# Combining a token's two expert rows: one plain gather added by PE with the identity, one adding gather onto LN1 output loaded at the 25th expert

## The chip, the cores and the metric

The kernel runs on 1 core of one Trainium2 chip. The metric is device time in microseconds (us), lower is better. Three runs of the kernel before gave 1243.73, 1244.65 and 1237.64 us: median 1243.73.

## The reference, cut to what matters

One decoder layer over 1024 tokens (and 16 meta tokens) of width 1024: a token mixer (stick-breaking attention beside a gated delta rule), a LayerNorm (LN1), then a mixture of experts and a second LayerNorm (LN2). Each token goes to the best 2 of 8 experts inside the best 1 of 4 groups, so to 2 of 32 experts:

```python
h = layer_norm(DEEPNORM_ALPHA * h + mix, ln1_g[i], ln1_b[i])
ffn = hierarchical_moe(h.reshape(b * l, D_MODEL), ...)   # sum over a token's two experts of
                                                         # gate * (silu(x @ w1) * (x @ w3)) @ w2
h = layer_norm(DEEPNORM_ALPHA * h + ffn, ln2_g[i], ln2_b[i])
```

All is float32. The part that the change touches is the sum of a token's LN1 output `h`, its two expert rows, and the LN2 behind it.

## The kernel before

Up to some 810 us the kernel does the mixer, LN1 (its output goes to the DRAM buffer `h1d`) and the routing. Then `phase4` runs over the 32 experts, `e` = 0 to 31, in an order written out by hand (`manual_schedule`), and `finish` does the combination and LN2 for 8 tiles of 128 tokens, `t` = 0 to 7.

**Experts.** An expert has up to 128 token slots. Its tokens are gathered from `h1d` by an indirect DMA on POOL (L1499, three experts ahead), transposed on PE, multiplied with w1 and w3 (`up`: the float32 pieces 6 and 7 straight from the loaded weights on L1527, the others as a high and a low part, L1531 to L1533), and with w2 (`down`, L1559 to L1561). ACT and DVE split each loaded weight piece into its two parts (L1462, L1463). The result, times the gate, is stored to the DRAM buffer `ysd` (`keep`, L1572, on POOL) for experts 0 to 29; the rows of the last two experts stay in SBUF (`ys`) and are brought to their tokens by PE with 0/1 matrices `oh` in `finish`.

**Weights.** `load_raw` (L1437) issues the 96 weight loads of 1 MiB on SP's queue: for each expert two halves of w1 and w3, then w2. They go round a ring of 17 buffers: 4 of a pool left over from the mixer (`wo4h`, `wo4l`, `wo6h`, `wo6l`), RA = 5 (`rawa`), RB = 6 (`rawb`), RC = 2 (`rawc`). A load into a buffer waits until the load of 17 before it has been split. L1630 keeps the ring full at the end of each expert.

**Combination.** `rb.close()` (L1641) frees `rawb` and `rawc` behind the loop, and the pool `fin` takes their place. Into it SP loads the 8 tiles `yts[t]` from `h1d` (L1648) and the LN2 gain and bias `g2`, `b2` (L1650). POOL then issues, for t below GE = 5, two indirect gathers with an add for each tile (`combine`, L1574 to L1578): row k = 0 and row k = 1 of each token from `ysd`, both added by the DMA onto `yts[t]`:

```python
for k in range(2):
    nc.gpsimd.indirect_dma_start(out=yts[t], ..., in_=src, in_offset=...fi[:, t, k:k + 1]..., compute_op=ALU.add)
```

Both write the same tile, so the second waits until the first has landed. `fi` (L1603) holds the row numbers; a row out of bounds is skipped. The call of `overflow` (L1664) is a branch taken only when an expert has more than 128 tokens; inside it `yts` is written too.

**finish.** For each tile: `total` (PE brings the last two experts' rows into PSUM, `pf`; DVE adds `yts[t]`, L1773), `square` (ACT), `rstd` (DVE L100 and POOL L101), `shift` (which first issues the gathers of tile t + GE through `more`, then L1785), `scale` (ACT L119), `gain` (DVE L1791), `store` (DVE L1794, then the DMA out, L1795). The order is by `t + TO[i]` with the offsets `TO = (0, 0.75, 1.25, 2.5, 3.25, 4, 4.75)` (L37, L1798): `total(4)` stands ahead of `gain(0)` and `rstd(3)`, and so on. POOL's queue in `finish` is: rstd(0), rstd(1), gathers of tile GE, rstd(2), gathers of tile GE + 1, rstd(3), and on.

Of the kernel before, what the change touches and what calls it, by code (L numbers as in the profile page):

```python
# [8 lines left out]
F32 = mybir.dt.float32  # L9
# [3 lines left out]
ALU = mybir.AluOpType  # L13
# [33 lines left out]
YB = 2  # L47
GE = 5
SPK = ()
# [9 lines left out]
MB, BB, WB, TB = 2, 2, 2, 3  # L59
RA, RB, RC = 5, 6, 2  # L60
RT = 2
GB = 3 * HA * DH
# [18 lines left out]
class Trunk:  # L81
# [738 lines left out]
    def phase2(self):  # L820
# [241 lines left out]
        self.h1d = self.dram.tile([SEQ, D], F32, name="h1d")  # L1062
        self.ysd = self.dram.tile([(NE - 2) * P, D], F32, name="ysd")
        self.ovd = self.dram.tile([16 * P, D], F32, name="ovd")
# [372 lines left out]
    def load_raw(self, n=1, eng=None):  # L1437
        order = [(0, 0), (0, 1)] + [w for e in range(1, NE) for w in ((e, 0), (e, 1), (e - 1, 2))] + [(NE - 1, 2)]
        for _ in range(n):
            i = len(self.raws)  # L1440
            if i == 3 * NE:
                return
            j = i % (RA + RB + 4 + RC) - 4
            if j < 0:
                raw = self.wp.tile([P, 4, 512], F32, name=f"wo{8 + j // 2 * 2}{'hl'[j % 2]}")
            else:
                k = 0 if j < RA else 1 if j < RA + RB else 2
                raw = self.rawp[k].tile([P, 4, 512], F32, name="raw", bufs=(RA, RB, RC)[k])
            e, c = order[len(self.raws)]
            (eng or self.nc.sync).dma_start(raw, self.a["w13"][e][:, c * 4:c * 4 + 4] if c < 2 else self.a["w2"][e])  # L1450
            self.raws[e, c] = raw
# [23 lines left out]
    def phase4(self):  # L1475
# [9 lines left out]
        for i in range(XN):  # L1485
            x = xp.tile([P, D], F32, name=f"xg{i}")
            nc.scalar.activation(x, self.ones[:, 0:1].to_broadcast([P, D]), AF.Copy, scale=0.0)
            XB.append(x)

        def loads(w13, w2):  # L1490
# [82 lines left out]

        def combine(src, fi, n, t):  # L1574
            for k in range(2):
                nc.gpsimd.indirect_dma_start(out=yts[t], out_offset=None, in_=src,  # L1576
                                             in_offset=bass.IndirectOffsetOnAxis(ap=fi[:, t, k:k + 1], axis=0),
                                             bounds_check=n * P - 1, oob_is_err=False, compute_op=ALU.add)  # L1578

# [5 lines left out]

        pcs = {0: self.pcs0}

        def gat_(e):
# [13 lines left out]
        nc.vector.tensor_scalar(fo, self.pose, float(P), 4096.0, op0=ALU.is_ge, op1=ALU.mult)  # L1602
        nc.vector.tensor_tensor(fi, fv, fo, op=ALU.add)  # L1603
        xt = xsplit(xpose(XB[0]))
        gat_(XN)
        self.load_raw(2 + RC - RX)
        for e in range(NE):
# [12 lines left out]
            else:  # L1620
# [8 lines left out]
                evac2(yo, self.gsl[:, e - 1:e], ys[0])  # L1629
            self.load_raw(max(0, 5 + 3 * e + RA + RB + 4 + RC - len(self.raws)))  # L1630
            if e == NE - 6:
# [7 lines left out]
            if e == NE - 2:  # L1639
                oh = [xp.tile([P, NT, P], F32R, name=f"xg{i}") for i in (2, 0)]  # L1640
        self.rb.close()  # L1641
        fin = ExitStack()
        fp = fin.enter_context(self.pool("fin", "left"))
        g2, b2 = [fp.tile([P, D], F32, name=n) for n in ("g2", "b2")]
        ys.append([fp.tile([P, D], F32R, name=f"y{x}") for x in "hl"])
        yts = [fp.tile([P, D], F32, name=f"yt{t}") for t in range(NT)]
        for t in range(NT):
            nc.sync.dma_start(yts[t], self.h1d[t * P:(t + 1) * P, :])  # L1648
        for v, n in ((g2, "ln2_g"), (b2, "ln2_b")):
            nc.sync.dma_start(v, self.bcast(a[n], D))  # L1650
        for t in range(GE):
            combine(self.ysd, fi, NE - 2, t)
        evac2(down(act, pcs.pop(NE - 1)), self.gsl[:, NE - 1:], ys[1])
# [9 lines left out]

        self.overflow(item, ps, fp.tile([P, D], F32, name="xo"), combine)  # L1664
        pss.close()
        sq = mp.tile([P, KT, P], F32R, name="xh", bufs=1).rearrange("p a b -> p (a b)")
        self.finish(fp, g2, b2, yts, oh, ys, sq, lambda t: t < NT and combine(self.ysd, fi, NE - 2, t))
        fin.close()
        es.close()
        self.wos.close()  # L1670

    def overflow(self, item, ps, xo, combine):
        nc, tc, a = self.nc, self.tc, self.a
        nv = nc.values_load(self.nov[0:1, 0:1], min_val=0, max_val=16)
        pose, oh, val, slots, ob, nx = self.pose, self.oh, self.val, self.slots, self.ob, self.nx
        with tc.If(nv > 0), self.pool("ovf", "left") as vp:
# [63 lines left out]
            with tc.For_i(0, nv) as i:  # L1740
# [7 lines left out]
                     xi, xg, xo, yi)  # L1748
            for t in range(NT):
                combine(self.ovd, fi, 16, t)  # L1750

    def finish(self, fp, g2, b2, yts, oh, ys, sq, more):
        nc, tc = self.nc, self.tc
        st = [fp.tile([P, 4], F32, name=f"st{t}") for t in range(NT)]
        rs = [fp.tile([P, 2], F32, name=f"rs{t}") for t in range(NT)]
        with self.psum("psf") as ps, tc.manual_schedule():
            pfs = {}

            def part(t, j0):
                if j0 == 0:  # L1760
                    pfs[t] = ps.tile([P, D], F32, name="pf", bufs=4)
                for c in range(2):
                    for j in (j0, j0 + 1):
                        nc.tensor.matmul(pfs[t][:, c * 512:(c + 1) * 512], oh[j // 2][:, t],
                                         ys[j // 2][j % 2][:, c * 512:(c + 1) * 512], start=(j == 0), stop=(j == 3))

            part(0, 0)
            part(1, 0)
            def total(t):
                if t > 1:  # L1770
                    part(t, 0)
                part(t, 2)
                nc.vector.scalar_tensor_tensor(yts[t], pfs.pop(t), 1.0, yts[t], op0=ALU.mult, op1=ALU.add,  # L1773
                                               accum_out=st[t][:, 0:1])
# [84 lines left out]
```

## Time and profile before

| | |
|---|---|
| median of three runs | 1243.73 us (1237.64 to 1244.65) |
| the profiled execution's own time | 1243.68 us |
| its span in the trace | 1241.9 us |
| busy in the span: PE, DVE, ACT, POOL | 1079.4, 863.0, 631.0, 292.4 us |
| q1 (SP's DMA queue), share of the 16 DMA engines | 55.5% |
| q0 (POOL's DMA queue), share of the 16 DMA engines | 8.9% |

The times of rows are from the span's start; 1.8 us of the execution's own time lie outside the span. Busy shares are means over stages that differ: the expert loop runs from some 820 to 1130 us, the combination behind it to the end. `<-` behind an idle time names what ended it.

### The profile page before, as it was taken

The numbers are of one execution on the slowest core, as the hardware profiler recorded it, in microseconds if no ns is written. First come the engines' busy times: TensorE is split into PE (matmuls) and PEld (weight loads), VectorE is DVE, ScalarE is ACT, GpSimd is POOL, SyncE is SP. The second block draws the span as 40 slices with busy tenths as digits, with TensorE's granted clock in tenths as the row PEclk, the third lists the DMA queues.
The fourth block names the chain that finished last, engine by engine and source line by source line (L and its number), as shares of the span: only waits on it lengthen the run. The fifth ranks groups of instructions, "written<-read, shape, count | busy, mean of one in ns | idle before, by whom it ended". The sixth has DMA issues, their size and how long they took to land. (4 is left out here: it accounts for less than half of the span.)

```text
span 1241.9 us, 19751 instructions
## 1 busy us (share of the span) xinstructions
PE 1079.4 (87%) x7029; PEld 930.2 (75%) x7029; DVE 863.0 (69%) x1671; ACT 631.0 (51%) x1310; POOL 292.4 (24%) x389
## 2 busy tenths in 40 slices
PE   6999999999899988989899998579999999996030
PEld 5999999999799867777677777457777777774020
DVE  7931358988232378989577777869999999994045
ACT  3443437754233345655365542347777777772042
POOL 3523003402000033344243220021111111203331
PEclk8999999999899978999899997879999999999565
DMA  8411124485985676874675717669999999934645
GB/s 282 175 54 44 60 91 121 136 247 174 251 233 163 229 247 203 231 240 127 190 184 138 276 69 295 227 234 385 401 396 401 400 405 412 376 147 133 105 83 152
DMA packets 112439, 270.74 MB, mean 218 GB/s; under 512 B 31140, under 2 KB 60588, under 8 KB 99538
## 3 DMA queue, kind: packets, MB, share of 16 engines
q1 hardware_dynamic: 100816, 236.43, 55.5%
q0 software_dynamic: 11232, 31.95, 8.9%
q8 instruction: 57, 0.93, 0.3%
q10 hardware_dynamic: 290, 1.07, 0.2%
q14 instruction: 44, 0.36, 0.1%
HBM read 213.83 MB, written 64.53 MB: 224 GB/s over the span
## 5 line engine op out<-in xcount | busy, mean ns | idle before, releaser
L185 PE MATMUL pj<-hTh,wfh 128*128 128x346 f32 (+1 forms) x480 | 156.2, 325 | 0.0
L186 PE MATMUL pj<-hTl,wfh 128*128 128x346 f32 (+1 forms) x480 | 155.7, 324 | 0.0
L187 PE MATMUL pj<-hTh,wfl 128*128 128x346 f32 (+1 forms) x480 | 155.7, 324 | 0.0
L880 DVE TENSOR_TENSOR_SCAN mm<-mm,zero 128x272 f32<-128x272 f32 (+3 forms) x64 | 89.5, 1412 | 23.1 <-ACT mm L867 21.0
L185 PEld LDWEIGHTS pj<-hTh,wfh 128*128 128x128 f32 x480 | 90.8, 189 | 0.4 <-issue 0.2
L186 PEld LDWEIGHTS pj<-hTl,wfh 128*128 128x128 f32 x480 | 90.8, 189 | 0.2
L187 PEld LDWEIGHTS pj<-hTh,wfl 128*128 128x128 f32 x480 | 90.8, 189 | 0.1
L1463 DVE TENSOR_TENSOR w13l<-raw,w13h 128x512 fp32r<-128x512 f32 x144 | 88.8, 684 | 0.0
L1531 PE MATMUL ph<-w13h,xh 128*128 128x512 f32 x192 | 88.3, 460 | 0.0
L178 PE MATMUL pj<-wvh,hTl 128*128 128x256 f32 (+3 forms) x280 | 79.6, 287 | 2.6 <-DVE hTl L96 2.6
L177 PE MATMUL pj<-wvl,hTh 128*128 128x256 f32 (+3 forms) x280 | 79.6, 287 | 2.2 <-DVE wvl L96 2.2
L176 PE MATMUL pj<-wvh,hTh 128*128 128x256 f32 (+3 forms) x280 | 80.0, 290 | 0.0
L1462 ACT ACTIVATE w13h<-raw 128x512 fp32r<-128x512 f32 x144 | 77.6, 619 | 0.0
L1533 PE MATMUL ph<-w13h,xl 128*128 128x512 f32 x192 | 75.1, 391 | 0.0
L1532 PE MATMUL ph<-w13l,xh 128*128 128x512 f32 x192 | 74.6, 389 | 0.0
L1499 POOL DMA_INDIRECT xg<-h1d,ix x32 | 34.0, 1063 | 170.5 <-PE tp L1509 133.3
L871 POOL TENSOR_SCALAR_AFFINE_SELECT mm<-mm 128x128 f32<-128x128 f32 x64 | 39.3, 619 | 115.4 <-ACT mm L867 115.2
L867 ACT ACTIVATE mm<-z 128x512 f32<-128x512 f32 (+1 forms) x80 | 44.3, 565 | 42.7 <-PE z L865 28.6
L865 PE MATMUL z<-qk 128*128 128x416 f32 (+6 forms) x224 | 60.9, 380 | 4.9 <-ACT kuw L777 2.1
L1463 DVE TENSOR_TENSOR w2l<-raw,w2h 128x512 fp32r<-128x512 f32 x96 | 59.9, 687 | 2.1
L95 ACT ACTIVATE xh<-tp 128x512 fp32r<-128x512 f32 x64 | 31.5, 492 | 50.2 <-DVE xf L1518 43.2
L178 PEld LDWEIGHTS pj<-wvh,hTl 128*128 128x128 f32 (+1 forms) x280 | 52.7, 188 | 3.5 <-DVE hTl L96 3.1
(428 smaller groups left out, 2924.1 us busy)
## 6 DMA issues: line engine op xcount, KB each, us to landing
raw<-in_w SPq DMA_DIRECT2D x72, 1024.0 KB, 13.8
ysd<-y POOLq DMA_DIRECT2D x30, 512.0 KB, 8.5
qk<-qkd SPq DMA_DIRECT2D x16, 520.0 KB, 5.4
ht<-hscr SPq DMA_DIRECT2D x16, 512.0 KB, 3.3
qk<-qkd SPq DMA_DIRECT2D x16, 392.0 KB, 7.1
kqvd<-y SPq DMA_DIRECT2D x12, 520.0 KB, 2.8
wfr<-in_w_gdn SPq DMA_DIRECT2D x12, 512.0 KB, 3.6
wo4l<-in_w SPq DMA_DIRECT2D x6, 1024.0 KB, 9.4
```

What stands on the lines that cost most here:

```text
L176: nc.tensor.matmul(o[:p, :n], xh, wh[:, kt, ws], start=(kt == 0), stop=False)
L177: nc.tensor.matmul(o[:p, :n], xh, wl[:, kt, ws], start=False, stop=False)
L178: nc.tensor.matmul(o[:p, :n], xl, wh[:, kt, ws], start=False, stop=(kt == KT - 1))
L185: nc.tensor.matmul(o[:, :n], wh[:, kt], self.hTh[:, kt, c0:c0 + n], start=(kt == 0), stop=False)
L186: nc.tensor.matmul(o[:, :n], wh[:, kt], self.hTl[:, kt, c0:c0 + n], start=False, stop=False)
L187: nc.tensor.matmul(o[:, :n], wl[:, kt], self.hTh[:, kt, c0:c0 + n], start=False, stop=(kt == KT - 1))
L880: nc.vector.tensor_tensor_scan(mm[:, c0:c1][:, ::-1], mm[:, c0:c1][:, ::-1], self.zero1.to_broadcast([P, c1 - c0]), 1.0, op0=ALU.mult, op1 ...
L1462: nc.scalar.activation(wh, raw, AF.Copy)
L1463: (nc.gpsimd if k in pool else nc.vector).tensor_tensor(wl, raw, wh.bitcast(F32), op=ALU.subtract)
L1531: nc.tensor.matmul(ph, xh[:, kt], wh, start=False, stop=False)
L1532: nc.tensor.matmul(ph, xh[:, kt], wl, start=False, stop=False)
L1533: nc.tensor.matmul(ph, xl[:, kt], wh, start=False, stop=(kt == ks[-1]))
```

## The change

Of a token's two rows from `ysd`, row k = 1 is now gathered plainly into a buffer of its own, `ybs[t]`, and PE adds it to `pf` in PSUM by two float32 matmuls with the identity. Row k = 0 is still added by the DMA onto `yts[t]`. The plain gather can't skip a row, so `fi` is cut to a row of zeros at the end of `ysd`, written once by ACT's queue. The 8 `ybs` tiles lie in the four `wo` buffers. `yts` is loaded from `h1d` at the end of expert e = FE = 24, which needs the place of `rawb` and `rawc` by then: from load RL = 77 on the weight ring has 9 buffers (4 `wo`, 5 `rawa`) in place of 17. GE goes from 5 to 4. In `overflow` the order of the gathers changes (k outside, t inside).

```diff
-GE = 5
+GE = 4
+FE, RL = NE - 8, 4 * (RA + RB + 4 + RC) + 4 + RA
...
-        self.ysd = self.dram.tile([(NE - 2) * P, D], F32, name="ysd")
+        self.ysd = self.dram.tile([(NE - 2) * P + 1, D], F32, name="ysd")
...
-            j = i % (RA + RB + 4 + RC) - 4
+            j = i % (RA + RB + 4 + RC) - 4 if i < RL else (i - RL) % (RA + 4) - 4
...
+        nc.scalar.dma_start(self.ysd[(NE - 2) * P:, :], XB[XN - 1][:1, :])
...
+        def combine(src, fi, n, t, k, o, **kw):
+            nc.gpsimd.indirect_dma_start(out=o, out_offset=None, in_=src,
+                                         in_offset=bass.IndirectOffsetOnAxis(ap=fi[:, t, k:k + 1], axis=0),
+                                         bounds_check=n - 1, oob_is_err=False, **kw)
+
+        def rows(t):
+            combine(self.ysd, fi, (NE - 2) * P + 1, t, 1, ybs[t])
+            combine(self.ysd, fi, (NE - 2) * P, t, 0, yts[t], compute_op=ALU.add)
...
-        nc.vector.tensor_tensor(fi, fv, fo, op=ALU.add)
+        nc.vector.tensor_tensor(fv, fv, fo, op=ALU.add)
+        nc.vector.tensor_scalar(fi, fv, float((NE - 2) * P), None, op0=ALU.min)
...
-            self.load_raw(max(0, 5 + 3 * e + RA + RB + 4 + RC - len(self.raws)))
+            n = 5 + 3 * e + RA + 4
+            self.load_raw(max(0, min(n + RB + RC, max(n, RL)) - len(self.raws)))
+            if e == FE:
+                self.rb.close()
+                fp = fin.enter_context(self.pool("fin", "left"))
+                yts = [fp.tile([P, D], F32, name=f"yt{t}") for t in range(NT)]
+                for t in range(NT):
+                    nc.sync.dma_start(yts[t], self.h1d[t * P:(t + 1) * P, :])
...
-        self.rb.close()
...
-        yts = [fp.tile([P, D], F32, name=f"yt{t}") for t in range(NT)]
-        for t in range(NT):
-            nc.sync.dma_start(yts[t], self.h1d[t * P:(t + 1) * P, :])
+        ybs = []
+        for w in ("4l", "6h", "6l", "4h"):
+            yb = self.wp.tile([P, 4, F], F32, name="wo" + w).rearrange("p (t a) f -> p t (a f)", t=2)
+            ybs += [yb[:, i] for i in range(2)]
...
         for t in range(GE):
-            combine(self.ysd, fi, NE - 2, t)
+            rows(t)
...
-                                         ys[j // 2][j % 2][:, c * 512:(c + 1) * 512], start=(j == 0), stop=(j == 3))
+                                         ys[j // 2][j % 2][:, c * 512:(c + 1) * 512], start=(j == 0), stop=False)
...
                 part(t, 2)
+                for c in range(2):
+                    ns = slice(c * 512, (c + 1) * 512)
+                    nc.tensor.matmul(pfs[t][:, ns], self.ident, ybs[t][:, ns], start=False, stop=True)
```

## Rows read from the trace of the kernel before

**Rows 1.** Windows: us, busy by engine (count), granted clock, DMA share, GB/s

```profile
1000.00:1030.00 30.00, 30.00 (x138) 23.03 (x137) 28.72 (x55) 22.60 (x45) 5.93 (x7) 1.00 1.01 406
...
1090.00:1120.00 30.00, 30.00 (x136) 22.56 (x135) 28.44 (x54) 23.35 (x48) 2.04 (x4) 1.00 0.27 106
...
1150.00:1185.00 35.00, 1.67 (x4) 1.38 (x5) 2.56 (x6) 1.63 (x5) 8.86 (x6) 0.50 0.57 98
```

**Rows 2.** Waits from 1100 us on: who waited for whom, us, times, longest

```profile
POOL yt L1576 <- DMA yt<-ysd,fi: 53.0, 8, 9.4
```

**Rows 3.** Timeline of POOL behind the loop: start us, us, what [idle before <-releaser]

```profile
1123.65 4.92 POOL L1576 DMA_INDIRECT yt<-ysd,fi  x1 [3.49 <-issue]
1138.01 1.58 POOL L1576 DMA_INDIRECT yt<-ysd,fi  x1 [9.44 <-DMA yt<-ysd,fi]
1139.89 1.56 POOL L1576 DMA_INDIRECT yt<-ysd,fi  x1 [0.30 <-issue]
...
1147.61 1.56 POOL L1576 DMA_INDIRECT yt<-ysd,fi  x1 [6.16 <-DMA yt<-ysd,fi]
...
1175.65 1.56 POOL L1576 DMA_INDIRECT yt<-ysd,fi  x1 [5.82 <-DMA yt<-ysd,fi]
```

**Rows 4.** Line view of L1676, the overflow branch: ns min/median/max, first and last start

```profile
L1676 POOLq EVENT_SEMAPHORE  x5: 17/43/43, 1176.5 to 1181.6; - x5
```

**Rows 5.** Timeline of finish: DVE and POOL, cut

```profile
1182.04 1.22 DVE L1773 SCALAR_TENSOR_TENSOR yt<-pf,yt 128x1024 f32<-128x1024 f32 x1 [48.63 <-DMA yt<-ysd,fi]
...
1187.29 1.61 POOL L1576 DMA_INDIRECT yt<-ysd,fi  x1 [0.33 <-issue]
...
1196.24 2.65 POOL L1576 DMA_INDIRECT yt<-ysd,fi  x1 [0.18 <-issue]
...
1200.09 1.22 DVE L1773 SCALAR_TENSOR_TENSOR yt<-pf,yt 128x1024 f32<-128x1024 f32 x1 [2.69 <-DMA yt<-ysd,fi]
...
1207.02 1.15 POOL L101 TENSOR_TENSOR rs<-rs,mhalf 128x1 f32<-128x1 f32 x1
...
1224.72 1.23 DVE L1773 SCALAR_TENSOR_TENSOR yt<-pf,yt 128x1024 f32<-128x1024 f32 x1 [2.65 <-DMA yt<-ysd,fi]
...
1236.71 1.22 DVE L1794 TENSOR_TENSOR yt<-yt,b 128x1024 f32<-128x1024 f32 x1
```

**Rows 6.** DMA queues: packets, MB, share of 16 engines; windows 1122:1128 and 1138:1147

```profile
q1 hardware_dynamic: 215, 0.82, 36.5%
...
q0 software_dynamic: 288, 0.98, 64.3%
```

**Rows 7.** DMA issues, us to landing; issued at 1123.65, 1147.61, 818.63 and 1066.54

```profile
yt<-ysd,fi POOLq DMA_INDIRECT x1, 14.0
...
yt<-ysd,fi POOLq DMA_INDIRECT x1, 6.1
...
xg<-h1d,ix POOLq DMA_INDIRECT x1, 4.0
...
raw<-in_w SPq DMA_DIRECT2D x1, 1024.0 KB, 21.5
```

**Rows 8.** Timeline of SP's queue behind the loop

```profile
1125.62 0.43 SPq L1650 DMA_DIRECT2D g<-in_ln_g  x1
```

**Rows 9.** Timeline of POOL in the loop: two experts' gathers of tokens

```profile
1067.55 1.07 POOL L1499 DMA_INDIRECT xg<-h1d,ix  x1 [5.29 <-PE tp L1509]
...
1077.21 1.07 POOL L1499 DMA_INDIRECT xg<-h1d,ix  x1 [5.29 <-PE tp L1509]
```

**Rows 10.** Timelines of PE (expert 28) and ACT (first split of expert 31)

```profile
1089.39 1.88 PE L1527 MATMUL ph<-raw,xf 128*128 128x512 f32 x4
...
1111.33 3.23 ACT L1462 ACTIVATE w13h<-raw 128x512 fp32r<-128x512 f32 x6
```

**Rows 11.** Timeline of PE: last matmul ahead of its wait, first one behind it

```profile
1141.31 0.40 PE L1764 MATMUL pf<-yl,xg 128*128 128x512 f32 x1
...
1183.33 0.80 PE L1764 MATMUL pf<-y,xg 128*128 128x512 f32 x1 [41.62 <-DVE yt L1773]
```

More of the change, by code (lines that the diff above doesn't have):

```diff
@@ L1572, in keep, with over @@
             nc.gpsimd.dma_start(self.ysd[e * P:(e + 1) * P, :], y)
-        def combine(src, fi, n, t):
+        def combine(src, fi, n, t, k, o, **kw):
[5 more added lines that the diff above has]
+            combine(self.ysd, fi, (NE - 2) * P, t, 0, yts[t], compute_op=ALU.add)
+        def over(fi):
             for k in range(2):
-                nc.gpsimd.indirect_dma_start(out=yts[t], out_offset=None, in_=src,
-                                             in_offset=bass.IndirectOffsetOnAxis(ap=fi[:, t, k:k + 1], axis=0),
-                                             bounds_check=n * P - 1, oob_is_err=False, compute_op=ALU.add)
+                for t in range(NT):
+                    combine(self.ovd, fi, 16 * P, t, k, yts[t], compute_op=ALU.add)
         def evac2(yo, gv, y):
@@ L1586, in phase4 @@
         pcs = {0: self.pcs0}
+        fin = ExitStack()
         def gat_(e):
@@ L1629, in phase4 @@
                 evac2(yo, self.gsl[:, e - 1:e], ys[0])
-            self.load_raw(max(0, 5 + 3 * e + RA + RB + 4 + RC - len(self.raws)))
+            n = 5 + 3 * e + RA + 4
[4 more added lines that the diff above has]
+                yts = [fp.tile([P, D], F32, name=f"yt{t}") for t in range(NT)]
+                for t in range(NT):
+                    nc.sync.dma_start(yts[t], self.h1d[t * P:(t + 1) * P, :])
             if e == NE - 6:
@@ L1640, in phase4 @@
                 oh = [xp.tile([P, NT, P], F32R, name=f"xg{i}") for i in (2, 0)]
-        self.rb.close()
-        fin = ExitStack()
-        fp = fin.enter_context(self.pool("fin", "left"))
         g2, b2 = [fp.tile([P, D], F32, name=n) for n in ("g2", "b2")]
         ys.append([fp.tile([P, D], F32R, name=f"y{x}") for x in "hl"])
-        yts = [fp.tile([P, D], F32, name=f"yt{t}") for t in range(NT)]
-        for t in range(NT):
-            nc.sync.dma_start(yts[t], self.h1d[t * P:(t + 1) * P, :])
+        ybs = []
+        for w in ("4l", "6h", "6l", "4h"):
+            yb = self.wp.tile([P, 4, F], F32, name="wo" + w).rearrange("p (t a) f -> p t (a f)", t=2)
+            ybs += [yb[:, i] for i in range(2)]
         for v, n in ((g2, "ln2_g"), (b2, "ln2_b")):
@@ L1662, in item @@
                                          in_=y, in_offset=None, bounds_check=16 * P - 1, oob_is_err=False)
-        self.overflow(item, ps, fp.tile([P, D], F32, name="xo"), combine)
+        self.overflow(item, ps, fp.tile([P, D], F32, name="xo"), over)
         pss.close()
         sq = mp.tile([P, KT, P], F32R, name="xh", bufs=1).rearrange("p a b -> p (a b)")
-        self.finish(fp, g2, b2, yts, oh, ys, sq, lambda t: t < NT and combine(self.ysd, fi, NE - 2, t))
+        self.finish(fp, g2, b2, yts, oh, ys, sq, ybs, lambda t: t < NT and rows(t))
         fin.close()
@@ L1670, in phase4, with overflow @@
         self.wos.close()
-    def overflow(self, item, ps, xo, combine):
+    def overflow(self, item, ps, xo, over):
         nc, tc, a = self.nc, self.tc, self.a
@@ L1748, in overflow, with finish @@
                      xi, xg, xo, yi)
-            for t in range(NT):
-                combine(self.ovd, fi, 16, t)
-    def finish(self, fp, g2, b2, yts, oh, ys, sq, more):
+            over(fi)
+    def finish(self, fp, g2, b2, yts, oh, ys, sq, ybs, more):
         nc, tc = self.nc, self.tc
```

## The prediction

> **What bounds the kernel now.** I read the windows first, to find where the end is set. In the expert loop PE is busy throughout at the full clock (1.00, 2.4 GHz), and the DMA engines are full as well (share 1.01) until the weights are in; after 1090 us they are nearly free (0.27) [rows 1]. Behind the loop no engine is busy: from 1150 to 1185 us PE works 1.67 us and POOL 8.86 us of 35 [rows 1]. So the loop is bound by PE, the tail by a wait. The waits from 1100 us on name it: POOL stands 53.0 us for the adding gathers into `yt` [rows 2]. POOL's timeline shows the pattern: a gather of tile t, then idle until it lands, the second gather of the same tile, 0.30 us later the first of the next tile, and so on, 9.6 us a tile (1138.01 to 1147.61), five tiles, the last issue at 1175.65 [rows 3]. DVE could start `total(0)` with its tile long complete, but at the branch of `overflow` POOL waits until 1181.6 for every gather in flight [rows 4], and DVE's first L1773 comes at 1182.04 [rows 5]. In `finish` three tiles more are gathered in the same way; the last `total` starts at 1224.72 and the end is 17.2 us behind it (1241.9) [rows 5].
>
> **The sum is made against the profiled execution**: span 1241.9 us, with 1.8 us around it 1243.68, practically the median of the runs shown (1243.73).
>
> **Early gathers (`rows(t)` in place of two adds, GE 4 for 5).** The two gathers of a tile no longer write the same place, so nothing orders them; nor do the `yts` loads hold them, since they are in long before. What remains is the issue on POOL and the transfer.
> - Start: 1123.65, as now, since it waits for the same last store into `ysd`. The first issue took 4.92 us there [rows 3]; a plain gather in the loop took 1.07 [rows 9]. I keep 4.92, because DVE's work beside it is the same: 1128.6.
> - Transfer: two adding gathers held 64.3% of 16 engines for 9 us, so 2.9 us each; plain loads moved 0.82 MB in 36.5% of 6 us, so 1.4 us for a plain 0.52 MB [rows 6]. A pair is 4.3 us. Issuing a pair takes 1.07 + 1.57 + 2 x 0.30 = 3.2 us [rows 3, 9], so transfer sets the pace: four pairs, 17.2 us.
> - Fixed part: a lone adding gather landed 6.1 us from its issue [rows 7], 1.57 of it issue and 2.9 transfer, so 1.6 more. Last landing 1128.6 + 17.2 + 1.6 = 1147.4; with 0.4 us from landing to DVE [rows 4, 5], `total(0)` starts at **1147.8** in place of 1182.04: **34.2 us gained**.
> - The first gather's landing of 14.0 us [rows 7] goes too: the loads of `g2` and `b2` that now sit beside it (SP issues them at 1125.62, behind `yts` loads that wait for buffers [rows 8]) are issued in the loop, for SP no longer waits ahead of them.
> - Bounds: if the first issue takes 1.07 us and issue sets the pace, four pairs end at 1123.65 + 13.0 = 1136.6, and with the remaining 4.5 us of the last landing and 0.4 us it is 1141.5 (40.5 gained). If all later seven issues take the 2.65 us seen at 1196.24 [rows 5] plus 0.30, it is 1123.65 + 4.92 + 20.7 + 4.9 = 1154.2 (27.8 gained).
>
> **The same in `finish`.** Call the start of `total(0)` T. Tile 4's pair is issued at T + 5.25 (1187.29 against 1182.04 [rows 5]), its adding gather 1.4 us later, landing 6.1 behind that: `total(4)` at T + 12.7. Tile 5's pair follows on POOL behind 1.07 + 0.30 + 1.57 + 0.30 of issue and one L101 of 1.15 with 0.2 of handing over [rows 3, 5, 9], so at T + 9.9: landed at T + 17.4. Tile 6's pair is behind rstd(3), which DVE does behind `total(4)` and `gain(0)`, 1.22 us each [rows 5], then L101: T + 16.5, landed T + 24. Tile 7's, in the same way behind `total(5)`: T + 21.2, landed T + 28.7; one us more for a slow issue (2.65 for 1.57), since each later tile shows one [rows 5]: `total(7)` at T + 29.7. Now it is T + 42.7 (1224.72). **13.0 us gained** (bounds below).
>
> **The identity matmuls.** Two float32 matmuls of 512 columns: on L1527 two such took 1.88 us at full clock [rows 10], 3.8 at half. They come behind the plain gather, which lands 4.0 us from its issue [rows 7]; the adding one lands 1.4 + 6.1 = 7.5 us from the same point. So the cover is 3.5 us: at full clock the matmuls are free, at half clock they end some 0.3 us late. If half clock holds for all, tile 5's eight `oh` matmuls (0.43 us apiece at half clock: 3.4) and its identity queue behind tile 4's, and `total(5)` slips by some 3 us, `total(7)` to T + 34. PE stops at 1141 and is at half clock at 1183 (0.80 for 0.40 us [rows 11]); now it has gaps of some 6 us, so I take the cover as holding, and keep 4.3 us for the range.
>
> **The loop: 9 weight buffers from load 77, and 4 MB of `yts` at e = 24.** A load now waits for the split of the load 9, not 17, before it: eight loads, 8/3 of an expert's 9.66 us [rows 9], so some 26 us later. The tightest is a second half of w1 and w3, whose buffer is held until L1527 has read it: that of expert 31 may be issued when expert 28's is free, 1089.39 + 1.88 = 1091.3, and is first split at 1111.33 + 4/6 of 3.23 = 1113.5 [rows 10]: 22.2 us of lead. Loads landed up to 21.5 us from their issue at the end of the loop [rows 7], with some 20 us of other loads queued ahead. The pause of 26 us empties that queue; `yts` then puts 4.2 MB at 406 GB/s, 10.3 us, into it [rows 1]. So I expect landings of 15 to 19 us, no wait, and cost **0**. SP stands longer in its queue; what is behind it is only later weights, `g2` and `b2`. Bound: 21.5 + 10.3 = 31.8 us against 22.2, so 9.6 us late; below, nothing, for PE has no idle time to give back.
>
> **The rest.** One DVE instruction on 16 numbers, a 4 KB store on ACT's queue ahead of the third token gather (needed two experts later): under 0.2 us, taken as 0. Work behind `total(7)` has the same order: 17.2 us.
>
> **Sum:** 1241.9 - 34.2 - 13.0 = 1194.7, with 1.8 around it **1196 us**.
>
> **Rivals.**
> - *The tail runs slower than its cover.* Half clock for the identities gives +4.3; issues of 2.65 us throughout give +6.4 on T. For it: 2.65 at 1196.24, with DVE's gain and store instructions beside it [rows 5]. Against: pairs at 1.56 to 1.58 us where DVE was idle [rows 3]. 1199 to 1207 us.
> - The Trainium skill's page SBUF — State Buffer (section Who interferes with whom) speaks for this rival: a DVE instruction with two SBUF inputs contends with a GpSimd instruction that reads SBUF, and the one that comes second is blocked until the first ends. The 2.65 against 1.57 us agrees with it; by it early issues under DVE's last splits would all be slow.
> - *The loop starves.* Weights come up to 9.6 us late: 1197 to 1206 us. For it: the DMA share of 1.01 [rows 1]. Against: the lead above.
> - *Slower than before.* The same starvation, where PE stands long enough for its clock to fall as it did in its wait of 41.6 us [rows 11]: each expert then costs another 9.66 us. From about five experts at half clock the 47 us are gone; with six (26 to 31) it is 1196 + 58 = 1254 us. It decides only if the lead of 22.2 us is missed again and again; DMA has room after 1090 [rows 1].
> - *The change doesn't do what it says.* If a pair still goes one after the other (a wait left between the two, or between tiles that share a buffer), four tiles take 4 x 9.6 + 3.4 of the slow first issue, T is 1165.9, and `finish` is as now: 1241.9 - 16.1, with 1.8: 1227.6 us. Against: gathers into different tiles are issued 0.30 us apart now [rows 3].
>
> The Trainium skill's page DMA: Bandwidth & Descriptors (section Anatomy of one DMA) has 2.0 us plus bytes at 436 GB/s for a DMA of POOL's, 3.2 us for one tile; the 6.1 us of the adding gather is far above it, the measurement decides. By the page four pairs would move in 9.6 us, an estimate, issue would set the pace, and the sum would be some 1190.
>
> **How the numbers follow.** Forecast 0.62 (its own range 1188 to 1200: T at its early bound and no slow issue gives 1196.5 - 6.3 - 1.0 = 1189); slower tail 0.2; starved loop 0.1; pairs still in series 0.05; clock lost 0.02; 0.01 for the unforeseen. The range 1188 to 1209 takes in the first two and most of the third, with some 0.15 left out. A measurement here can tell about 1%, 12.4 us, from no change. All cases but the last two end below 1231: faster 0.95, same 0.03, slower 0.02.
>
> **What would show it.** Right: POOL's eight early gathers 1.4 to 2 us apart with no idle time for a DMA between the two of a tile; DVE's first `total` near 1148, its last about 30 us behind it; PE's windows in the loop still full from 1060 to 1120. Wrong: PE idle on a weight piece in the last experts (starved); identity matmuls ending behind the adding gather's landing (clock); POOL still idle for `yt` between pairs (in series).

## The result

The changed kernel took **1201.05 us** (median of 4 runs, 1195.57 to 1204.54) against 1242.88 for the kernel before in the same comparison: a ratio of **0.967** (95% interval 0.962 to 0.971), 41.8 us faster. The forecast was 1196 us, its range 1188 to 1209. The profiled execution took 1195.57 us, with a span of 1193.8.

The windows of the kernel after (us, busy by engine with counts, granted clock, DMA share, GB/s), against [rows 1]:

```profile
1060.00:1090.00 30.00, 30.00 (x138) 23.00 (x137) 28.77 (x54) 23.63 (x49) 7.08 (x11) 1.00 1.02 403
1090.00:1120.00 30.00, 30.00 (x138) 23.03 (x137) 28.71 (x53) 23.51 (x48) 1.61 (x3) 1.00 0.88 368
1120.00:1150.00 30.00, 24.31 (x90) 16.11 (x89) 13.66 (x26) 8.68 (x18) 12.76 (x11) 1.00 0.59 137
1150.00:1185.00 35.00, 16.31 (x40) 8.17 (x40) 19.25 (x31) 15.72 (x23) 18.10 (x14) 0.76 0.73 190
```

The loop is as full as before (PE 30.00 of 30 us up to 1120); the DMA share of 1090 to 1120 rose from 0.27 to 0.88, since the weights that stood behind `yts` in SP's queue now land there, and `g2` and `b2` with them. From 1150 to 1185, where PE had worked 1.67 us, it works 16.31.

POOL's timeline after (start us, us, what, idle before and its releaser), against [rows 3, 5]:

```profile
1121.07 1.27 POOL L1579 DMA_INDIRECT wo4l<-ysd,fi  x1 [3.48 <-issue]
1122.65 1.99 POOL L1579 DMA_INDIRECT yt<-ysd,fi  x1 [0.30 <-issue]
1124.93 1.02 POOL L1579 DMA_INDIRECT wo4l<-ysd,fi  x1 [0.30 <-issue]
...
1132.62 1.56 POOL L1579 DMA_INDIRECT yt<-ysd,fi  x1 [0.30 <-issue]
...
1149.34 1.06 POOL L1579 DMA_INDIRECT wo6l<-ysd,fi  x1 [0.48 <-issue]
...
1153.06 1.05 POOL L1579 DMA_INDIRECT wo6l<-ysd,fi  x1 [0.18 <-issue]
...
1161.71 1.05 POOL L1579 DMA_INDIRECT wo4h<-ysd,fi  x1 [0.18 <-issue]
...
1166.89 1.05 POOL L1579 DMA_INDIRECT wo4h<-ysd,fi  x1 [0.18 <-issue]
```

The waits of 5.8 to 9.4 us between the two gathers of a tile are gone: eight issues, each 0.30 us behind the one before. The pairs of tiles 4 to 7 start at 1149.34, 1153.06, 1161.71 and 1166.89. DVE's timeline has the totals of tiles 0 and 4 to 7, and the last instruction of the end:

```profile
1143.93 1.23 DVE L1794 SCALAR_TENSOR_TENSOR yt<-pf,yt 128x1024 f32<-128x1024 f32 x1 [13.29 <-DMA yt<-ysd,fi]
...
1157.46 1.23 DVE L1794 SCALAR_TENSOR_TENSOR yt<-pf,yt 128x1024 f32<-128x1024 f32 x1 [7.64 <-PE pf L1793]
...
1162.63 1.23 DVE L1794 SCALAR_TENSOR_TENSOR yt<-pf,yt 128x1024 f32<-128x1024 f32 x1 [1.54 <-DMA yt<-ysd,fi]
...
1170.21 1.23 DVE L1794 SCALAR_TENSOR_TENSOR yt<-pf,yt 128x1024 f32<-128x1024 f32 x1 [3.94 <-DMA yt<-ysd,fi]
...
1176.65 1.23 DVE L1794 SCALAR_TENSOR_TENSOR yt<-pf,yt 128x1024 f32<-128x1024 f32 x1 [2.81 <-PE pf L1793]
...
1188.65 1.22 DVE L1815 TENSOR_TENSOR yt<-yt,b 128x1024 f32<-128x1024 f32 x1
```

`total(0)` starts at 1143.93 (1182.04 before) and `total(7)` at 1176.65, 32.7 us behind it (42.7 before).

**The marks used below.** The profiled executions of the kernels of this study start expert 1 up to 13 us apart (its first matmul at 820.7 to 833.7 us), though little of their code differs ahead of it, so absolute times don't compare. The loop itself, from expert 1's first matmul to expert 31's, took 289.90 to 290.05 us wherever it was read off, in the kernel before too. So I compare three stretches: from the start of the first early gather to `total(0)` ("early"), from `total(0)` to `total(7)` ("finish"), and the rest to the end.

| kernel | median us | ratio to before (95%) | early | finish | rest |
|---|---|---|---|---|---|
| before | 1242.88 | | 58.39 | 42.68 | 17.22 |
| after | 1201.05 | 0.967 (0.962–0.971) | 22.86 | 32.72 | 17.17 |
| after, again (e1) | 1199.61 | 0.966 (0.963–0.969) | 25.43 | 33.09 | 17.17 |
| e2, early load at 29th expert | 1201.38 | 0.967 (0.965–0.970) | 25.11 | 33.21 | 17.17 |
| e3, GE 5 | 1195.18 | 0.964 (0.961–0.967) | 28.58 | 25.39 | 17.17 |
| e4, both rows adding | 1234.63 | 0.995 (0.992–0.997) | 44.85 | 50.28 | 17.16 |
| e5, `yts` loaded behind the loop | 1201.10 | 0.968 (0.965–0.971) | 25.40 | 33.97 | 17.17 |
| e6, no identity matmuls | 1197.27 | 0.966 (0.962–0.969) | 24.52 | 32.78 | 17.17 |
| e7, both rows plain, no LN1 output | 1185.54 | 0.955 (0.952–0.959) | 18.94 | 29.13 | 17.16 |
| e8, GE 6 | 1193.38 | 0.963 (0.960–0.966) | 32.30 | 21.80 | 17.17 |
| e9, stores held back | 1194.38 | 0.962 (0.956–0.968) | 25.42 | 31.84 | 17.17 |
| e10, late compares | 1198.64 | 0.965 (0.960–0.970) | 22.54 | 34.05 | 17.17 |
| e11, both plain, LN1 output by PE | 1201.12 | 0.968 (0.964–0.973) | 24.78 | 36.12 | 17.16 |
| e12, both plain, LN1 output by DVE | 1188.33 | 0.957 (0.953–0.961) | 20.19 | 27.26 | 17.17 |

(For e12 early ends with the first of DVE's two additions of tile 0, and finish with the second of tile 7. The medians of before in the later comparisons were 1240.72 for e1 to e4, 1239.53 for e5 to e8, 1241.3 for e9 to e11, 1240.94 for e12. Two slow runs, one of e11 (1271.96 us) and one of the kernel before beside it (1663.9 us), both at a lower granted clock, are left out of these medians. All marks come from one profile of each kernel.)

### The profile page after: what moved, and what is told of

Its sections match the earlier page's. It is cut to its first block, busy times and chain, and to the rows that moved or that the text cites. A ratio compares the mean times of both kernels' runs of the same rounds, so it can differ in the third digit from the quotient of the medians.

```text
span 1193.8 us, 19810 instructions
## 1 busy us (share of the span) xinstructions
PE 1092.8 (92%) x7061; PEld 933.7 (78%) x7061; DVE 863.3 (72%) x1672; ACT 631.2 (53%) x1310; POOL 287.0 (24%) x389
## 4 chain that ended last, share of the span: by engine, by line
PE 70%; DMA 12%; DVE 9%; issue 4%; ACT 3%; POOL 1%; SPq 0%; POOLq 0%; DVEq 0%; ACTq 0%
PE pj L186 6%; PE pj L187 6%; PE pj L188 6%; PE ph L1531 5%; PE ph L1535 3%; PE ph L1537 3%; PE ph L1536 3%; DMA wst<-in_w_out 3%; PE pj L179 3%; PE pj L177 3%; PE pj L178 3%; DMA yt<-ysd,fi 2%; PE tp L1513 2%; PE pv L921 2%; PE py L1565 2%
## 5 line engine op out<-in xcount | busy, mean ns | idle before, releaser
L1465 DVE TENSOR_TENSOR w13l<-raw,w13h 128x512 fp32r<-128x512 f32 x126 | 77.8, 683 | 0.0
L1464 ACT ACTIVATE w13h<-raw 128x512 fp32r<-128x512 f32 x126 | 68.0, 620 | 0.0
L902 ACT ACTIVATE wt<-tp 128x512 f32<-128x512 f32 (+1 forms) x80 | 41.6, 556 | 27.6 <-PE tp L901 27.0
## 6 DMA issues: line engine op xcount, KB each, us to landing
wo4h<-in_w SPq DMA_DIRECT2D x8, 1024.0 KB, 13.5
```

The source lines that it names most:

```text
L1464: nc.scalar.activation(wh, raw, AF.Copy)
L1465: (nc.gpsimd if k in pool else nc.vector).tensor_tensor(wl, raw, wh.bitcast(F32), op=ALU.subtract)
```

## The experiments

**The same kernel again (e1), and the early load four experts later (e2).** The median lay 5 us above the forecast, and the profiled execution at it. Two theories: late weights cost some executions time (S), or the executions differ ahead of the loop or behind it (V). e2 loads `yts` four experts later, behind the last weight; the ring keeps its 9 buffers from load 77 on:

```diff
-FE, RL = NE - 8, 4 * (RA + RB + 4 + RC) + 4 + RA
+FE, RL = NE - 4, 4 * (RA + RB + 4 + RC) + 4 + RA
```

> The changed kernel once more, beside the other three. In its profiled execution (1195.57 us) a half of expert 30's weights landed 0.32 us before its first split, and ACT waited 0.6 us for a half of expert 29's; its other executions took 1199.8, 1202.3 and 1204.5 us. Theory S (weights come late in the slower executions): about 1201 us in the median, with executions between 1195 and 1206; where the profiled one is a slow one, PE shows idle time on weight pieces in experts 29 to 31. Rival V (the executions differ ahead of the loop or behind it): the same times, and a slow profile has its loss there.

> Only change: yts is loaded at the end of expert 28, behind the last weight load, in place of expert 24; the weight ring stays at 9 buffers from load 77. Theory S: the 4 MB no longer stand ahead of the weights of experts 28 to 31, so their slack rises from 0 to 2 us to about 8 us, no execution waits, and the median falls by 4 to 6 us, to 1195 to 1197. The tail stays as it is: the yts loads are issued at about 1093 and in by about 1115 to 1120, ahead of the first adding gather at 1122. Rival V: 1200 to 1202 as for the changed kernel.

1199.61 and 1201.38 us: no gain from the later load, and the loop takes the same 289.9 us in the profiles of after, e1 and e2. S falls. What differs lies outside the loop, as V has it: e2's profile starts expert 1 3.5 us later than e1's. The two profiles of the changed kernel itself start it within 0.4 us of each other (825.88 and 825.53); their 2.6 us of difference in span are in the early part. Of the other timed executions no profile shows where they differ.

**One tile more ahead of `finish` (e3).**

```diff
-GE = 4
+GE = 5
```

> Only change: GE = 5 in place of 4, so five pairs are issued ahead of the overflow branch and three in finish. If transfer sets the pace (4.3 us a pair), total(0) comes 3 to 4 us later, but rstd(3) no longer stands behind a total that waits for a gather, so tile 7's pair is issued some 8 us earlier against total(0): total(0) to the last total falls from 32.7 us to about 23, net 5 us faster than the changed kernel. Rival: the chain of gathers in finish is hidden by DVE's own 3.5 us a tile, and the later start makes it 3 to 4 us slower.

1195.18 us, 4.4 under the changed kernel beside it. Early grew by 3.15 us, finish shrank by 7.70, to 25.39 where I had expected about 23: a pair is cheaper where pairs follow one another at once than where each waits for `rstd` of an earlier tile. By the marks GE = 4, a part of the change, was itself a loss of some 4.5 us; the intervals of the two ratios overlap (0.961 to 0.967 and 0.963 to 0.969), so the runs don't show it by themselves.

**Both rows by adding DMAs again, with everything else of the change (e4).**

```diff
-            combine(self.ysd, fi, (NE - 2) * P + 1, t, 1, ybs[t])
+            combine(self.ysd, fi, (NE - 2) * P, t, 1, yts[t], compute_op=ALU.add)
...
-                for c in range(2):
-                    ns = slice(c * 512, (c + 1) * 512)
-                    nc.tensor.matmul(pfs[t][:, ns], self.ident, ybs[t][:, ns], start=False, stop=True)
```

> Undoes one part of the change: both rows of a token are added by the DMA onto yts, one after the other, and the identity matmuls are gone; yts is still loaded at expert 24 and GE is 4. Theory I (the gain is the independence of a tile's two gathers): four tiles at 9.6 us and finish at its old 42.7 us, about 1223 to 1228, some 25 us over the changed kernel. Rival E (the gain is the earlier load of yts, g2 and b2, which takes the 14 us landing of the first gather and the branch's wait away): at most 10 us over the changed kernel.

1234.63 us: of some 41 us only 6 are left. POOL's timeline shows the old pattern, a wait for the landing in front of every second gather:

```profile
1128.87 4.74 POOL L1579 DMA_INDIRECT yt<-ysd,fi  x1 [3.49 <-issue]
1138.97 1.58 POOL L1579 DMA_INDIRECT yt<-ysd,fi  x1 [5.36 <-DMA yt<-ysd,fi]
1140.86 1.56 POOL L1579 DMA_INDIRECT yt<-ysd,fi  x1 [0.30 <-issue]
1148.32 1.56 POOL L1579 DMA_INDIRECT yt<-ysd,fi  x1 [5.90 <-DMA yt<-ysd,fi]
```

So some 35 us of the gain are the independence of a tile's two gathers. Of the 6 us that are left, 4 stand at the first landing: POOL waits 5.36 us for it in front of the second gather, where it waited 9.44 [rows 3], with the loads of `yts`, `g2` and `b2` now in long before. My 1223 to 1228 us was too low because I left `finish` as it was: with GE = 4 four tiles go through the chain there, not three (50.28 us, before 42.68).

**The early load undone alone (e5).** `yts`, `g2` and `b2` are loaded behind the loop as before, the ring keeps 17 buffers to the end, and the pairs stay independent (the four `wo` buffers are also taken in another order):

```diff
-FE, RL = NE - 8, 4 * (RA + RB + 4 + RC) + 4 + RA
+FE, RL = NE - 8, 3 * NE
...
-            if e == FE:
-                self.rb.close()
...
+        self.rb.close()
+        fp = fin.enter_context(self.pool("fin", "left"))
...
+        for t in range(NT):
+            nc.sync.dma_start(yts[t], self.h1d[t * P:(t + 1) * P, :])
```

> Undoes the other part of the change: yts, g2 and b2 are loaded behind the loop again and the weight ring has 17 buffers to the end; the plain gather and the identity stay, GE is 4. Theory L (the early load is worth only the congestion around the first gathers): SP's yts loads 6 and 7, g2 and b2 are issued at about 1125 in DMA time that the early pairs want (2.1 MB, 5 us), so from the first gather to total(0) it takes 29 to 31 us in place of the 25.4 of the changed kernel run again, and the median is 3 to 6 us over it, 1203 to 1206. Rival N (the early load brings nothing, its loss in the loop eats it): within 2 us of the changed kernel, 1198 to 1202.

1201.10 us and an early part of 25.40 against 25.43, as rival N had it. Nothing measurable comes from loading LN1's output at the 25th expert. The last two tiles of it, issued at 1123.65 and 1124.02 here, do slow the first gather beside them (with `g2` and `b2` behind them): it landed 10.7 us from its issue, and 7.7 us in e9, which loads early and has the same slow first issue:

```profile
wo4h<-ysd,fi POOLq DMA_INDIRECT x1, 10.7
```

```profile
wo4l<-ysd,fi POOLq DMA_INDIRECT x1, 7.7
```

But no later gather waits for that landing any more. So the early load is worth 4 us where the pairs go in series (e4), and nothing where they are independent.

**The identity matmuls left out, and row 1 with them (e6).**

```diff
...
-                for c in range(2):
-                    ns = slice(c * 512, (c + 1) * 512)
-                    nc.tensor.matmul(pfs[t][:, ns], self.ident, ybs[t][:, ns], start=False, stop=True)
```

> Leaves out PE's identity matmuls, so row k = 1 is gathered but not added (part of the sum is left out). Theory D (the tail waits for the transfers): from the first to the last total 31 to 32 us in place of 33.1, so 1 to 2 us less, since the last identity ended 1.7 us behind the last adding gather. Rival P (half clock: the identities set the pace of finish): 28 to 30 us, 3 to 5 us less, near the 29.7 that was forecast.

The finish took 32.78 us against 33.09 with them in e1: 0.3 us, which is within the 0.5 us by which the same finish differs between the profiles of after, e1 and e2 (32.72 to 33.21). Early was 0.9 us shorter too; why, isn't shown. PE's timeline after shows two of the four of `finish`:

```profile
1153.64 3.78 PE L1793 MATMUL pf<-wo6l,ident 128*128 128x512 f32 x4 [5.80 <-DMA wo6l<-ysd,fi]
...
1173.97 2.65 PE L1793 MATMUL pf<-wo4h,ident 128*128 128x512 f32 x4 [3.99 <-DMA wo4h<-ysd,fi]
```

Tile 4's pair of matmuls took 3.78 us at half clock (1.98 for tiles 5 and 6) and ended 0.2 us behind its adding gather's landing at 1157.2 (issued at 1150.71, 6.5 us): the cover was all used, hardly exceeded.

**Both rows gathered plainly (e7).** Row 0 overwrites the LN1 output, which is left out of the sum:

```diff
-            combine(self.ysd, fi, (NE - 2) * P, t, 0, yts[t], compute_op=ALU.add)
+            combine(self.ysd, fi, (NE - 2) * P, t, 0, yts[t])
```

> Row k = 0 is gathered plainly too, over yts, so LN1's output is left out of the sum; all else as in the changed kernel. It measures what the add in the DMA costs. Theory T (transfer sets the pace, 2.9 us for an adding tile against 1.4): a pair takes 2.8 us of transfer, so the early part, first gather to total(0), falls from 25.4 to about 19 to 20 us, bound by issue; finish, first to last total, falls from 33.1 to about 28. About 10 us under the changed kernel. Rival Q (issue on POOL sets the pace): the early part stays at 23 us or more, finish at 31 or more.

Early fell to 18.94 us, finish to 29.13, 10.5 us together, as expected; the median lies 14 to 16 us under those of the changed kernel (e1 and after), and what the rest of that is, the marks don't show. The share of POOL's DMA queue in the windows from first gather to `total(0)`, eight gathers each, gives the price of a tile (packets, MB, share of 16 engines): after, 23 us (1121 to 1144),

```profile
q0 software_dynamic: 1152, 4.05, 75.8%
```

both rows adding (e4), 45 us (1129 to 1174),

```profile
q0 software_dynamic: 1152, 3.93, 52.5%
```

and both plain (e7), 19 us (1120 to 1139):

```profile
q0 software_dynamic: 1152, 4.05, 59.8%
```

That is 17.4, 23.6 and 11.4 us of transfer: 4.36 for a pair of one each, 2.95 for an adding gather, 1.42 for a plain one. All three agree with the 4.3, 2.9 and 1.4 of the forecast.

**Six tiles ahead of `finish` (e8).** `GE = 6` in place of 4.

> GE = 6. With GE = 5 the early part took 28.6 us and the first to last total 25.4 (25.4 and 33.1 with GE = 4), median 4.4 us less. Theory D: one pair more ahead of the branch adds 3.5 to 4 us (32.3), and the two pairs left are issued behind shift(0) and shift(1), ahead of any total that waits, so the last total comes about 18 us behind the first: sum 50.5 against 54.0, median 1191 to 1193. Rival: DVE's own work, 3.5 us a tile, becomes the bound and the sum stays at 53 to 55: 1195 to 1197.

Early 32.30, finish 21.80: together 54.1, as with GE = 5 (54.0), where I had expected 4 us less in finish. The two kernels can't be told apart; one tile more in front now costs what it saves. The sum is the rival's, but not for its reason, since DVE was busy for 17.01 of 23 us (the window from 1152 to 1175):

```profile
1152.00:1175.00 23.00, 16.49 (x48) 10.15 (x48) 17.01 (x32) 15.56 (x26) 12.21 (x10) 0.87 0.58 155
```

`total(7)` waited for its adding gather; the issues of tile 7's pair, while DVE worked, took 2.08 and 2.49 us in place of 1.05 and 1.56.

**Output stores away from the last gathers (e9).** Finish was 3 us longer than forecast. The stores of tiles 0 to 2 are issued behind that of tile 3:

```diff
-                nc.sync.dma_start(self.out[0, t * P:(t + 1) * P, :], yts[t])
+                for i in () if t < 3 else (3, 0, 1, 2) if t == 3 else (t,):
+                    nc.sync.dma_start(self.out[0, i * P:(i + 1) * P, :], yts[i])
```

> The changed kernel with one thing else: the output stores of tiles 0 to 2 are issued behind that of tile 3, whose DVE work comes behind total(7), so that no output store runs beside the gathers of tiles 5 to 7 in finish. The changed kernel took 32.7 to 34.0 us from total(0) to total(7), where I had forecast 29.7. Theory O (the output stores of 0.5 MB apiece take part of the DMA engines while the last pairs land): 31.0 to 32.0 us. Theory Q (the pairs queue behind each other, and tile 4's and 5's alone make the loss): 32.7 to 33.5 as before. The end may come some us later behind total(7) in either case, since three stores more are then at the end; the mark is total(0) to total(7).

Finish 31.84 against 33.09, with `total(6)` at the same place in both (26.1 us behind `total(0)`): the 1.25 us are all at tile 7, whose adding gather landed 8.3 us from its issue at 1170.82 in e1,

```profile
yt<-ysd,fi POOLq DMA_INDIRECT x1, 8.3
```

and 7.3 us from its issue at 1167.98 in e9:

```profile
yt<-ysd,fi POOLq DMA_INDIRECT x1, 7.3
```

So some 1.25 of the 3 us are the stores, and the rest isn't. It is one profile of each, in which finish differs by up to 0.5 us without any change; the two timed runs are too few to show it in the median.

**DVE's two compares moved (e10).** In e1 the first early gather took 4.2 us to issue, as in seven of the eight other profiles with the compares in their old place and a plain gather first; the exception is the profile of after, with 1.27 us:

```profile
1120.71 4.18 POOL L1579 DMA_INDIRECT wo4l<-ysd,fi  x1 [3.45 <-issue]
```

DVE was busy with instructions on two SBUF inputs without a break up to 1123.94, the splits and then the compares that make `oh`, and the issue ended 0.95 us behind them:

```profile
1119.17 2.49 DVE L1465 TENSOR_TENSOR w13l<-wo4h,w13h 128x512 fp32r<-128x512 f32 x4
1121.58 2.36 DVE L1637 TENSOR_TENSOR xg<-slots,ixt 128x1024 fp32r<-128x1024 f32 x2
```

In the profile of after the gather began 0.84 us ahead of the compares (1121.07 against 1121.91), in e1 0.87 us: the start doesn't tell the two apart, and why POOL wasn't held there is open.

e10 has the compares behind the last expert's rows, and nothing else:

```diff
-                for i in (1, 0):
-                    nc.vector.tensor_tensor(oh[i], ..., op=ALU.is_equal)
...
         evac2(down(act, pcs.pop(NE - 1)), self.gsl[:, NE - 1:], ys[1])
+        for i in (1, 0):
+            nc.vector.tensor_tensor(oh[i], ..., op=ALU.is_equal)
```

> The changed kernel with DVE's two compares that make the 0/1 matrices (L1637, 1.2 us each) moved from behind expert 31's splits to behind the last expert's rows (L1596). In four of five executions of the changed kernel POOL's first early gather took 4.2 us to issue while these compares ran, and in one, where it began just before them, 1.3 us. Theory B (DVE's instructions with two SBUF inputs hold POOL's issue): first issue 1.0 to 2.2 us, first gather to total(0) 22 to 23.5 us in place of 25.1 to 25.4, and the kernel 2 to 3 us faster than the changed kernel's 1199.6 to 1201.1. Rival (the first gather is slow by itself, whatever DVE does): 4.2 us, 25.4 us, no change.

In e10 the first early gather is issued in

```profile
1117.10 1.91 POOL L1579 DMA_INDIRECT wo4l<-ysd,fi  x1 [3.45 <-issue]
```

while DVE's splits now end the run, at 1118.07:

```profile
1115.57 2.50 DVE L1465 TENSOR_TENSOR w13l<-wo4h,w13h 128x512 fp32r<-128x512 f32 x4
```

The end is again 0.94 us behind DVE's. (e11 and e12, which have the late compares too, took 1.91 and 1.90 us.) Early fell by 2.9 us to 22.54. So the compares, not the gather, made it slow. But finish rose to 34.05: tile 7's identity matmuls ran at a granted clock of 0.50, half speed, for 3.78 us and ended 1.4 us behind the adding gather's landing, and the median (1198.64, interval of the ratio 0.960 to 0.970) can't be told from the changed kernel's. What the early part gained was in part given back.

**What the runs point to (e11, e12).** Both rows plain, into five pairs of buffers that tile t + 5 uses again (four `wo` buffers and one of `rawa`), GE = 5, late compares. In e11 PE adds the LN1 output too:

```diff
+                for c in range(2):
+                    ns = slice(c * 512, (c + 1) * 512)
+                    nc.tensor.matmul(pfs[t][:, ns], self.ident, yts[t][:, ns], start=False, stop=False)
...
-                nc.vector.scalar_tensor_tensor(yts[t], pfs.pop(t), 1.0, yts[t], op0=ALU.mult, op1=ALU.add,
+                nc.vector.scalar_tensor_tensor(yts[t], pfs.pop(t), 1.0, ybs[t % GE][0], op0=ALU.mult, op1=ALU.add,
```

> What the runs so far point to, put together in one kernel: both rows are gathered plainly into buffers of their own (5 pairs, used again by tile t + 5), PE adds the LN1 output and row 1 with the identity (four matmuls a tile in place of two), DVE adds row 0 in total; GE = 5; the compares of the 0/1 matrices behind the last expert's rows. From the run with plain gathers and no LN1 output (first gather to total(0) 18.9, total(0) to total(7) 29.1, span 1184.9) and from GE 5 against 4 (early part longer by one pair of 2.6 to 2.7, finish shorter by 6.6 to 7.7): theory P (the transfer and the chain of pairs set the tail): early 19 to 21.5, finish 21.5 to 23, median 1177 to 1182. Rival (the LN1 output's identity matmuls, at half clock 3.8 us a tile, come on the path): finish 25 to 27, median 1183 to 1187.

1201.12 us, no better than the changed kernel: both of my ranges were too low. The window from 1135 us, when the early gathers had landed (the last at 1134.7), to `total(7)` shows PE full (41.52 of 42 us) at a clock of 0.96, and DVE's timeline shows a total every 5.29 us, each released by PE:

```profile
1135.00:1177.00 42.00, 41.52 (x116) 22.39 (x116) 16.48 (x32) 15.77 (x26) 12.37 (x12) 0.96 0.33 111
```

```profile
1155.52 1.23 DVE L1798 SCALAR_TENSOR_TENSOR yt<-pf,raw 128x1024 f32<-128x1024 f32 x1 [3.94 <-PE pf L1797]
...
1160.82 1.23 DVE L1798 SCALAR_TENSOR_TENSOR yt<-pf,wo4h 128x1024 f32<-128x1024 f32 x1 [3.93 <-PE pf L1797]
...
1166.10 1.23 DVE L1798 SCALAR_TENSOR_TENSOR yt<-pf,wo4l 128x1024 f32<-128x1024 f32 x1 [1.65 <-PE pf L1797]
```

`total(0)`, at 1140.58, was released by PE as well. I had looked at the identities as a delay behind a landing and hadn't added up PE's work a tile. e12 takes the LN1 output off PE (against e11, cut):

```diff
...
-                    nc.tensor.matmul(pfs[t][:, ns], self.ident, yts[t][:, ns], start=False, stop=False)
...
+                nc.vector.tensor_tensor(yts[t], pfs.pop(t), yts[t], op=ALU.add)
+                nc.vector.scalar_tensor_tensor(yts[t], ybs[t % GE][0], 1.0, yts[t], op0=ALU.mult, op1=ALU.add,
```

> As the kernel with both rows gathered plainly, GE = 5 and the late compares, but DVE adds the LN1 output in place of PE: behind row 1's identity one DVE addition of PSUM onto the LN1 output, then one of row 0 with the accumulated sum; PE has two identity matmuls a tile as in the changed kernel. In the kernel with the LN1 output on PE the totals came every 5.29 us, each released by PE, and PE worked 5.3 us a tile without a gap: PE was the bound. Theory P (with PE relieved the transfer sets the pace): its ten early gathers had landed 18.9 us from the first one's start; the first addition there plus 0.4, so about 19.3; from the first addition to the last total about 20 to 23 us; median 1177 to 1182. Rival D (DVE's two additions of 1.2 us a tile become the bound, since tiles 0 to 4 are all there at once): 25 to 28 us, median 1183 to 1187.

1188.33 us, ratio 0.957 (0.953 to 0.961): the fastest kernel here that computes the whole layer, some 11 us below the changed one. Now DVE is the bound, as the rival had it (its median, 1183 to 1187, was a little low): 26.07 us busy of 28 in its finish, and the first additions of tiles 5, 6 and 7 come 4.8 us apart, behind four instructions of 1.22 us each.

```profile
1144.00:1172.00 28.00, 23.00 (x75) 13.62 (x73) 26.07 (x40) 15.79 (x26) 13.88 (x12) 0.99 0.48 164
```

```profile
1160.60 1.22 DVE L1795 TENSOR_TENSOR yt<-pf,yt 128x1024 f32<-128x1024 f32 x1
...
1165.40 1.22 DVE L1795 TENSOR_TENSOR yt<-pf,yt 128x1024 f32<-128x1024 f32 x1
...
1170.21 1.22 DVE L1795 TENSOR_TENSOR yt<-pf,yt 128x1024 f32<-128x1024 f32 x1
```

## Why the prediction was right, and where it was off

**The mechanism** was right: the gathers of a tile, set free of one another, gave nearly all of the gain, and e4, which takes back just that, loses some 35 of the 41 us. "Pairs still in series" (1227.6) is what e4 shows, at 1234.6, and the changed kernel doesn't.

**The number** of the profiled execution (1195.57 against 1196; the forecast's terms add up to 1196.5) is met in part by luck: its loop started 2.6 us earlier than that of the profile before, so the first early gather came at 1121.07 in place of 1123.65; early was 1.3 us under its forecast, finish 3.0 us over. By e1's marks the change gains 33.0 us in early and 9.6 in finish, 42.6 us, where 34.2 and 13.0 were forecast, 47.2 us; the medians beside e1 differ by 41.1.

**Early part.** Forecast 24.15 us from the first gather to `total(0)`, measured 22.86 in the profiled execution and 25.1 to 25.4 in e1, e2 and e5. The term of the transfer (17.2 us for four pairs) was right to 0.2 (17.4). Two smaller ones were off, in opposite directions. The first issue was kept at 4.92 us, which was an adding gather's; the plain one in its place took 4.2, or 1.27 in the profiled execution, where it wasn't held. And transfer doesn't set the pace from the first pair to the last: the DMA strip of e1's window (1121 to 1146, 40 slices, busy tenths) has slices of 5 and 6 over the first gathers, while POOL still issues, and ebbs over three slices at the end:

```profile
DMA  0000000569959989969999999999999999631000
```

With the measured 4.18 the forecast's sum would be 23.4, so these part-full slices are put at some 2 us (25.43); that is argued from the strip.

**The 14.0 us of the first landing**, put down to the loads of `g2` and `b2` beside it: the reason is borne out as far as the loads behind the loop go together (the last two of `yts`, `g2` and `b2`), by 4.1 us of wait less in e4 and 3.0 us of landing more in e5. But it is worth nothing in the early part of the changed kernel: e5 leaves these loads where they were, its first landing is late, and its early part is the same.

**Finish** is the term that was mis-sized, 29.7 us forecast and 32.7 to 33.2 measured in after, e1 and e2. Its steps, from `total(0)` in the profiled execution:

| | pair issued, forecast | measured | total, forecast | measured |
|---|---|---|---|---|
| tile 4 | 5.25 | 5.41 | 12.7 | 13.5 |
| tile 5 | 9.9 | 9.13 | 17.4 | 18.7 |
| tile 6 | 16.5 | 17.8 | 24.0 | 26.3 |
| tile 7 | 21.2 | 23.0 | 29.7 | 32.7 |

I gave each pair the 7.5 us of a lone one. Tile 5's is issued 3.7 us behind tile 4's, under the 4.36 us that a pair's transfer takes, and took 9.6 us. `rstd` of tiles 3 and 4, on which the next pairs wait, is late by what `total(4)` and `total(5)` are late, 0.8 and 1.3 us, and one POOL instruction in it took 1.55 us where I had 1.15. Tile 7's pair took 9.8 us, of which some 1.25 are the output stores (e9). The one us that the forecast set aside for a slow issue of tile 7's didn't come (1.05 and 1.56 us), so without it the forecast of finish would have been 4 us under. I had priced transfers for the early part, where they queue, and forgotten the queue in `finish`.

**Identity matmuls at no cost**: right in the changed kernel, to 0.3 us (e6). The clock did fall: 0.66 granted in the window from 1150 to 1160, when PE had waited 5.80 us for a landing. The cover of 3.5 us held just that long. In e5 and e10, where tile 7's pair met half clock (3.78 us), it was exceeded by 1.4 us; in e10 the cover itself had shrunk to 2.5 us, since tile 7's plain gather landed 7.3 us from its issue, not 4.0, and its adding one 8.4.

**The loop at no cost**: right, and closer than I had it. PE never waited in 1060 to 1120, but the landings that I put at 15 to 19 us took 20.4 us for the load of expert 30's second half, issued at 1080.45,

```profile
raw<-in_w SPq DMA_DIRECT2D x1, 1024.0 KB, 20.4
```

so that it was there at 1100.9, 0.3 us ahead of ACT's first split of it:

```profile
1101.19 1.14 ACT L1464 ACTIVATE w13h<-raw 128x512 fp32r<-128x512 f32 x2
```

A load issued at 1084.35 took 22.6 us, and was in 1.8 us ahead of its first split. One other load came 0.6 us late for ACT; nothing of it reached PE:

```profile
ACT w13h L1464 <- DMA wo4l<-in_w: 0.6, 1, 0.6
```

The early load put the kernel this near to the starving rival and bought nothing for it (e5).

**The tail's rival** (slow issues under DVE's work) came true in its first issue. The Trainium skill's page SBUF — State Buffer, section Who interferes with whom, says that a GpSimd instruction that reads SBUF and comes second to a DVE instruction with two SBUF inputs is held until that one ends; e1 and e10 agree (4.18 and 1.91 us, each ending some 0.95 behind DVE's run). The profile of after doesn't (1.27 us), nor does an adding gather of e10, which took its usual 1.56 us from 1125.75 while the moved compares ran from 1125.73.

## What to carry to other kernels

Look in POOL's queue for two DMAs into one tile: where only the add orders them, a second buffer and an engine that is idle there can take the add, and the price of a pair falls from two latencies to its transfer (here from some 9.3 us to 4.4). Then add up, for each engine, the work that a tile now brings in the stretch: the same idea moved once too far made PE the bound (e11), and with DVE it paid (e12). A chain of transfers is priced with the queue that it stands in, also where the pairs look apart.

## What had not been expected of the hardware

- An adding indirect gather of 0.52 MB held the 16 DMA engines 2.95 us (e4), a plain one 1.42 (e7): adding costs twice the transfer. The forecast had it from two rows; e4 and e7 show it by itself.
- The issue of a plain indirect gather on POOL took 1.0 to 1.1 us with DVE idle, and as the first early gather some 4.2 us beside an unbroken run of DVE instructions with two SBUF inputs; it ended some 0.95 us behind the run's end. In one profile of nine, that of after, it took 1.27 us with the same run beside it.
- The loop's time repeats to 0.15 us in 290 over the profiles of all the kernels here, while its start differs by 13 us between them. Whether the start also makes the spread between executions of one kernel isn't shown: the one kernel with two profiles (after and e1) started within 0.4 us.
